# Row chunks of the adaLN product in pairs, with five places, and shift columns loaded two tiles ahead

## The chip, the cores and the metric

The kernel runs on one core of a Trainium2 chip. The metric is the time of one execution on the device in microseconds (us); the lower the better. TensorE (PE) multiplies matrices, VectorE (DVE), ScalarE (ACT) and GpSimd (POOL) work on vectors, SyncE (SP) issues transfers; DMA engines move the data.

## What is computed

Two decoder layers on 256 positions of width 2048, in float32. Layer 0 has a causal conformer convolution as token mixer, layer 1 a stick-breaking attention; both are followed by a gated MLP. Each part is normed, shifted, scaled and gated by numbers that a conditioning vector c gives through its own product (adaLN). What matters here is the middle of layer 0:

```python
def ada_ln(c, w, b):
    mod = jax.nn.silu(c) @ w + b
    shift, scale, gate = jnp.split(mod, 3, axis=-1)

def conformer_conv_module(h, ...):
    u = h @ pw1_w + pw1_b
    ...
    u = causal_depthwise_conv(u, dw_w, dw_b)
    u = jax.nn.silu(layer_norm(u, ln_g, ln_b))
    return u @ pw2_w + pw2_b
...
    x = x + gate * y
    shift, scale, gate = ada_ln(c, ffn_mod_w[i], ffn_mod_b[i])
    h = rms_norm(x, ffn_norm_g[i]) * (1.0 + scale) + shift
    x = x + gate * conv_ffn(h, ffn_up_w[i], ffn_dw_w[i], ffn_dw_b[i], ffn_down_w[i])
```

## The kernel before, in words

A large product is made of blocks of 128 x 128 weights. The weights are split in two parts, wh and wl, and so is the input (zh, zl in this stage), and each block takes three matmuls (L297 to L299) on 256 columns. Weights come in pieces of eight blocks (0.5 MB), loaded by SP (L225), split by ACT (L243) and DVE (L247). The stage of this study is pw2, the second product of the conv module, with 32 pieces, 768 matmuls. Its inputs are the 16 results of the conv (ys, tiles of 128 x 256): DVE subtracts the mean (L922), multiplies by the deviation (L923), ACT and DVE make zh and zl. The first eight output tiles run interleaved over the first twelve input tiles and are then finished one by one; the last eight run one by one. Finished output tiles are evicted by ACT (L941), added to x by DVE (L942), and squared and summed for the next norm by ACT (L392) and POOL (L396).

Beside it runs a filler, a generator that the loop over pieces advances by a step after each piece. It computes adaLN numbers that later stages need, in two ways. Row chunks, 128 x 2048 numbers (1 MB): a chunk is multiplied on PE by four matmuls of 32 columns by 512, on four column groups at once (L576; the trace shows two records for each), and its rows are turned and biased later (L592, L598). Forty chunks make the gate of layer 0's mixer (0 to 15), the scale of its MLP (16 to 31) and half its shift (32 to 39). Chunks 20 to 39 are loaded in the pw2 stage by POOL (L556), each when PE has read what was in its place. The places are tiles of 1 MB: three named mraw and one zrow, given out by number and capped. The other half of the shift is made from columns tiles (mraw, 1 MB, loaded by `mod_load`, L318), each multiplied with silu(c) and summed by DVE in one instruction (L330, 2.3 us).

A scheduler of the framework fixes one order of instructions per engine from the program's text; up to the end of the conv the order is written out by hand, and in pw2 it is the scheduler's. Each engine works through its list in order, so that a load on POOL's list waits for what stands ahead of it. A place is used again when the reading of it is over, by a semaphore.

Of the kernel before, what the change touches and what calls it, by code (L numbers as in the profile page):

```python
# [10 lines left out]
F32 = mybir.dt.float32  # L11
# [5 lines left out]
P = 128  # L17
# [14 lines left out]
MORE_ROWS = 4  # L32
SPLIT_ROWS = 3
ROWS = 2

ROWS_AT = {**{c: (11,) for c in (2, 4, 6, 8, 10, 12)}, 13: (16, 17), 14: (8, 12, 16), 15: (2, 13, 15, 17)}
ROWS_TAIL = 5

RATES = {"pw2": (1.0, 0.0), "up": (0.44, 0.25), "down": (0.5, 0.0), "qk": (0.3, 0.0), "v": (0.3, 0.0),
         "o": (0.45, -3.0), "up00a": (0.0, 0.0), "qk0a": (0.0, 0.0),  # L40
# [76 lines left out]
def hybrid_trunk(ctx: ExitStack, tc: tile.TileContext, cfg: Cfg, io: dict):  # L117
    nc = tc.nc
    D, T, H = cfg.D, cfg.T, cfg.H
# [198 lines left out]
    def mod_load(m, nb, own=False):  # L318

        v = mpool.tile([P, D], F32, name="mraw")  # L320
        src = io["mt_" + m][mt_at[m].index(nb) if m in mt_at else nb]
        if own:
            nc.gpsimd.dma_start(v, src)  # L323
        else:
            load(src, v)
        return v

    def mod_reduce(m, nb, v):

        nc.vector.tensor_tensor_reduce(out=v, in0=v, in1=csr, scale=1.0, scalar=0.0, op0=ALU.mult, op1=ALU.add,  # L330
                                       accum_out=macc[:, nb:nb + 1])
# [11 lines left out]
    def mod_part(m, part, first):  # L343
        ahead = []
        for nb in range(part * KD + first, (part + 1) * KD):
            ahead.append((nb, mod_load(m, nb)))
            if len(ahead) > 1:
                mod_reduce(m, *ahead.pop(0))
            yield
        mod_reduce(m, *ahead.pop(0))  # L350
        mod_sum(m, part * KD + first, KD - first)
        yield

    later = []

# [139 lines left out]
    with ExitStack() as cv:  # L495
# [39 lines left out]
        def load_rows(most=1):  # L535

            while row_chunks and most:
                n = nrow["n"]
                near = n < nrow["near"]
                home = row_homes[n] if near else ("zmm"[n % 3] if n < 8 * KD // 4 else "zm"[n % 2]) if "z" in cpar else "m"  # L540
                cap = {"m": 3 if near else 1 + (n < 8 * KD // 4), "r": MORE_ROWS, "w": SPLIT_ROWS, "z": 1}[home]
                if sum(t[1] == home for t in row_tiles) >= cap:
                    break
                m, c, k0 = row_chunks.pop(0)
                src = io["mr_" + m][mr_at[m].index(c), :, k0 * 512:(k0 + 4) * 512]
                if home == "w":
                    v = [w_pool.tile([P, PW], F32R, name=x).bitcast(F32) for x in ("wh", "wl")]
                    for i in range(2):
                        load(src[:, i * PW:(i + 1) * PW], v[i])
                    v = [v[g // 2][:, g % 2 * 512:(g % 2 + 1) * 512] for g in range(4)]  # L550
                else:
                    v = (cpool2.tile([P, 4 * 512], F32, name="mrow", bufs=MORE_ROWS) if home == "r" else
                         cpar["z"].tile([P, 4 * 512], F32, name="zrow") if home == "z" else
                         mpool.tile([P, 4 * 512], F32, name="mraw"))
                    if "z" in cpar:
                        nc.gpsimd.dma_start(v, src)  # L556
                    else:
                        load(src, v)
                    v = [v[:, g * 512:(g + 1) * 512] for g in range(4)]
                row_tiles.append((v, home))  # L560
                nrow["n"] += 1
                most -= 1

        def mod_rows():
# [4 lines left out]
            for m, c0, n, done in rows_of:  # L569
                ps = (psum_acc if m == "ffn0" and c0 else psum_a)() if n else None  # L570
                for i in range(n):
                    for k0 in range(0, KD, 4):
                        v = row_tiles.pop(0)[0]
                        first, last = i == 0 and k0 == 0, i == n - 1 and k0 + 4 >= KD
                        for g in range(4):
                            nc.tensor.matmul(ps[32 * g:32 * g + 32, :], hot[:, k0 + g, 31 - i:63 - i],  # L576
                                             v[g], start=first, stop=last,
                                             tile_position=(0, 32 * g))
                        load_rows()
                        if later and nrow["bias"]:  # L580
                            later.pop(0)()
                        if last:
                            rows = cpool.tile([P, 512], F32, name="rows")
                            nc.scalar.copy(rows, ps)
                        else:
                            yield
# [18 lines left out]
                yield  # L605

        def mods0():
            part = mod_part("ffn0", 0, 4 * cfg.rows0) if cfg.rows0 * 4 < KD else iter(())
            for _ in mod_rows():
                yield  # L610
                if ("ffn0", 1) in have and next(part, "end") != "end":
                    yield
            yield from part
            have.add(("ffn0", 0))

        gb = cpool.tile([P, KD], F32, name="gb")
        ready = {"k": 0}
        ys = [cpool.tile([P, T], F32, name=f"y{j}") for j in range(KD)]
        for kt in range(KD):
            nc.gpsimd.tensor_tensor(ys[kt], xs[kt], rs, op=ALU.mult)  # L620
        htiles = [h_tiles(kt) for kt in range(KD)]
# [678 lines left out]
```

## Time and profile before

| | us |
|---|---|
| median of three runs | 2310.33 (2307.93 to 2311.91) |
| the profiled execution | 2314.76 |
| its span, first to last instruction | 2313.1 |
| stage pw2 in it, first to last matmul | 286.5 to 408.9 |

The profile shows one execution. Its own time lies above the span by what is outside the first and last instruction. The rows below come from the page and from questions to its trace: timelines (one engine's instructions, with start, duration and in brackets the idle time ahead of it and what ended it), groups by line, waits, windows, and how long transfers took from issue to landing.

### The profile page before, as it was taken

What the parts mean: (1) busy time and instruction counts of PE and PEld (TensorE: products, weight loads), DVE (VectorE), ACT (ScalarE), POOL (GpSimd) and SP (SyncE); (2) the same over time, 40 slices, a digit from 0 to 9 for tenths busy, and PEclk for the clock granted to TensorE, in tenths of its full rate; (3) what the DMA queues carried; (4) which work ended last, traced back from release to release, by engine and by line L of the source; (5) the groups of instructions that cost most, each with busy time, mean ns of one, the idle gap of its engine ahead of it and who ended that gap; (6) DMA issues with size and microseconds to landing.
All of it is one profiled execution on the core that took longest, in us unless ns stands there. A gap on an engine that the chain in (4) does not pass through costs nothing.

```text
span 2313.1 us, 44241 instructions
## 1 busy us (share of the span) xinstructions
PE 2273.3 (98%) x17834; PEld 2170.2 (94%) x17834; DVE 1737.9 (75%) x2386; ACT 1163.5 (50%) x1776; POOL 334.4 (14%) x478
## 2 busy tenths in 40 slices
PE   7999999999999999999999999999999999999997
PEld 5888678999999999999999999999999999999997
DVE  7689968899998899998875555668666545666554
ACT  2056655755543355554465555647555434555543
POOL 4058713200001000001211000121000000000010
PEclk9999999999999999999999999999999999999999
DMA  9988798689999999998854555555555555555553
GB/s 394 417 323 308 272 370 350 236 319 362 344 362 386 361 343 358 348 357 329 330 182 164 165 172 174 164 191 177 189 191 186 189 187 187 190 186 190 188 186 110
DMA packets 139167, 603.56 MB, mean 261 GB/s; under 512 B 15441, under 2 KB 15569, under 8 KB 115153
## 3 DMA queue, kind: packets, MB, share of 16 engines
q1 hardware_dynamic: 120242, 464.42, 56.0%
q0 software_dynamic: 18720, 136.32, 15.8%
q8 instruction: 139, 2.28, 0.4%
q14 instruction: 66, 0.54, 0.1%
HBM read 598.58 MB, written 2.10 MB: 260 GB/s over the span
## 4 chain that ended last, share of the span: by engine, by line
PE 62%; issue 23%; DVE 5%; DMA 5%; POOL 2%; ACT 1%; POOLq 0%; SPq 0%; DVEq 0%; ACTq 0%
PE ps L297 17%; PE ps L298 17%; PE ps L299 16%; PE ps L663 5%; DMA mraw<-in_mt_mix 3%; POOL mraw L323 2%; DVE mraw L330 2%; DMA mraw<-in_mt_ffn 2%; DVE wl L247 1%; PE ps L1125 1%; PE ps L1127 1%; PE ps L1126 1%; PE ps L576 1%; PE auxa L576 1%; ACT hl L712 0%
## 5 line engine op out<-in xcount | busy, mean ns | idle before, releaser
L247 DVE TENSOR_TENSOR wl<-raw,wh 128x1024 fp32r<-128x1024 f32 x688 | 844.4, 1231 | 414.7 <-ACT wh L243 409.1
L243 ACT CAST wh<-raw 128x1024 fp32r<-128x1024 f32 x688 | 719.3, 1048 | 822.9 <-PE ps L298 645.9
L297 PE MATMUL ps<-hh,wh 128*128 128x256 f32 (+1 forms) x3264 | 915.8, 281 | 0.0
L298 PE MATMUL ps<-hl,wh 128*128 128x256 f32 (+1 forms) x3264 | 912.1, 279 | 0.0
L299 PE MATMUL ps<-hh,wl 128*128 128x256 f32 (+1 forms) x3264 | 908.3, 278 | 0.1
L298 PEld LDWEIGHTS ps<-hl,wh 128*128 128x128 f32 x3264 | 617.7, 189 | 0.3
L299 PEld LDWEIGHTS ps<-hh,wl 128*128 128x128 f32 x3264 | 612.8, 188 | 0.7 <-DVE wl L247 0.7
L297 PEld LDWEIGHTS ps<-hh,wh 128*128 128x128 f32 x3264 | 612.7, 188 | 0.3
L299 PE MATMUL ps<-gh,wl 128*128 128x256 f32 x1408 | 394.6, 280 | 7.1 <-DVE wl L247 7.1
L298 PE MATMUL ps<-gl,wh 128*128 128x256 f32 x1408 | 396.4, 282 | 0.0
L297 PE MATMUL ps<-gh,wh 128*128 128x256 f32 x1408 | 395.4, 281 | 0.0
L330 DVE CUSTOM_DVE_ANT_0 mraw<-mraw,csr 128x2048 f32<-128x2048 f32 x152 | 348.5, 2294 | 52.6 <-DMA mraw<-in_mt_mix 30.9
L299 PEld LDWEIGHTS ps<-gh,wl 128*128 128x128 f32 x1408 | 266.0, 189 | 8.1 <-DVE wl L247 8.1
L298 PEld LDWEIGHTS ps<-gl,wh 128*128 128x128 f32 x1408 | 266.9, 190 | 0.0
L297 PEld LDWEIGHTS ps<-gh,wh 128*128 128x128 f32 x1408 | 266.2, 189 | 0.0
L396 POOL TENSOR_TENSOR sumsq<-sumsq,t 128x256 f32<-128x256 f32 x56 | 65.0, 1162 | 885.8 <-ACT t L392 885.6
L663 PE MATMUL ps<-hh,raw 128*128 128x256 f32 x832 | 188.8, 382 | 0.0
L663 PEld LDWEIGHTS ps<-hh,raw 128*128 128x128 f32 x832 | 157.8, 191 | 28.3 <-issue 6.7
L964 DVE SCALAR_TENSOR_TENSOR t<-ps,par,t 128x254 f32<-128x254 f32 x328 | 157.1, 479 | 3.9
L703 DVE SCALAR_TENSOR_TENSOR auxb<-u,cpar,auxb 128x256 f32<-128x256 f32 x297 | 121.6, 483 | 4.5 <-ACT auxb L687 3.7
L838 POOL TENSOR_TENSOR y<-y,hl 128x256 f32<-128x256 f32 x143 | 104.4, 730 | 13.4 <-ACT hl L712 3.3
L961 ACT ACTIVATE t<-ps,par 128x256 f32<-128x256 f32 x164 | 91.8, 560 | 0.0
(247 smaller groups left out, 2271.3 us busy)
## 6 DMA issues: line engine op xcount, KB each, us to landing
raw<-in_w_down SPq DMA_DIRECT2D x176, 512.0 KB, 3.8
mraw<-in_mt_ffn POOLq DMA_DIRECT2D x64, 1024.0 KB, 8.3
raw<-in_w_pw SPq DMA_DIRECT2D x96, 512.0 KB, 7.9
mraw<-in_mt_mix POOLq DMA_DIRECT2D x48, 1024.0 KB, 8.1
raw<-in_w_up01b SPq DMA_DIRECT2D x84, 512.0 KB, 6.8
raw<-in_w_up11b SPq DMA_DIRECT2D x84, 512.0 KB, 3.5
raw<-in_w_up00b SPq DMA_DIRECT2D x80, 512.0 KB, 6.5
raw<-in_w_up10b SPq DMA_DIRECT2D x80, 512.0 KB, 3.5
```

What stands on the lines that cost most here:

```text
L243: nc.scalar.copy(wh[:, :n], v[:, :n])
L247: nc.vector.tensor_tensor(wl[:, :n], v[:, :n], wh[:, :n].bitcast(F32), op=ALU.subtract)
L297: nc.tensor.matmul(o, wh[:, c], xh[kt], start=first, stop=False, skip_group_check=halves > 0)
L298: nc.tensor.matmul(o, wh[:, c], xl[kt], start=False, stop=False, skip_group_check=halves > 0)
L299: nc.tensor.matmul(o, wl[:, c], xh[kt], start=False, stop=left[nb] == 0, skip_group_check=halves > 0)
L330: nc.vector.tensor_tensor_reduce(out=v, in0=v, in1=csr, scale=1.0, scalar=0.0, op0=ALU.mult, op1=ALU.add, accum_out=macc[:, nb:nb + 1])
L396: engine.tensor_tensor(self.sum, self.sum, sq, op=ALU.add)
L663: nc.tensor.matmul(banks[j][:, nb // KD * T:(nb // KD + 1) * T], w[:, b * P:(b + 1) * P], hf[kt], start=first, stop=left[j] == 0, skip_gro ...
L703: nc.vector.scalar_tensor_tensor(conv_ps[j], us[j % UBUFS][:, k:k + T], tap(j, k), conv_ps[j], op0=ALU.mult, op1=ALU.add)
L838: nc.gpsimd.tensor_tensor(ys[c], ys[c], pr, op=ALU.add)
L961: nc.scalar.activation(y, ps[:, :T], AF.Identity, bias=pc(f"fdb{i}", nb, 1), scale=w(FW - 1))
L964: nc.vector.scalar_tensor_tensor(y[:, s:], ps[:, :T - s], w(k), y[:, s:], op0=ALU.mult, op1=ALU.add)
```

## The change

The places of chunks 20 to 39 come from a string, `LATE_HOMES`, with one letter for each chunk: m (two tiles mraw), z (zrow), y (two halves of what held the conv's results). The results ys are now cut from two tiles of eight results, named yhalf, and a chunk with home y takes a half when its results have been read. In the pw2 stage the filler takes two row chunks at a step, and two loads are issued at a chunk in place of one; two columns tiles stand behind each pair once the scale is done. Columns tiles of the shift are loaded by POOL (`own=True`) in place of SP, and two tiles are in flight ahead of the one that is reduced, in place of one.

```diff
@@ -35,6 +35,8 @@
 
 ROWS_AT = {**{c: (11,) for c in (2, 4, 6, 8, 10, 12)}, 13: (16, 17), 14: (8, 12, 16), 15: (2, 13, 15, 17)}
 ROWS_TAIL = 5
+
+LATE_HOMES = "mmzyymmzyymzyyzyyzyy"
 
 RATES = {"pw2": (1.0, 0.0), "up": (0.44, 0.25), "down": (0.5, 0.0), "qk": (0.3, 0.0), "v": (0.3, 0.0),
          "o": (0.45, -3.0), "up00a": (0.0, 0.0), "qk0a": (0.0, 0.0),
@@ -343,13 +345,14 @@
     def mod_part(m, part, first):
         ahead = []
         for nb in range(part * KD + first, (part + 1) * KD):
-            ahead.append((nb, mod_load(m, nb)))
-            if len(ahead) > 1:
+            ahead.append((nb, mod_load(m, nb, own=True)))
+            if len(ahead) > 2:
                 mod_reduce(m, *ahead.pop(0))
+                yield
+        while ahead:
+            mod_reduce(m, *ahead.pop(0))
             yield
-        mod_reduce(m, *ahead.pop(0))
         mod_sum(m, part * KD + first, KD - first)
-        yield
 
     later = []
 
@@ -537,8 +540,8 @@
             while row_chunks and most:
                 n = nrow["n"]
                 near = n < nrow["near"]
-                home = row_homes[n] if near else ("zmm"[n % 3] if n < 8 * KD // 4 else "zm"[n % 2]) if "z" in cpar else "m"
-                cap = {"m": 3 if near else 1 + (n < 8 * KD // 4), "r": MORE_ROWS, "w": SPLIT_ROWS, "z": 1}[home]
+                home = row_homes[n] if near else LATE_HOMES[n - nrow["near"]] if "z" in cpar else "m"
+                cap = {"m": 3 if near else 2, "r": MORE_ROWS, "w": SPLIT_ROWS, "z": 1, "y": 2}[home]
                 if sum(t[1] == home for t in row_tiles) >= cap:
                     break
                 m, c, k0 = row_chunks.pop(0)
@@ -551,6 +554,7 @@
                 else:
                     v = (cpool2.tile([P, 4 * 512], F32, name="mrow", bufs=MORE_ROWS) if home == "r" else
                          cpar["z"].tile([P, 4 * 512], F32, name="zrow") if home == "z" else
+                         cpool.tile([P, 4 * 512], F32, name="yhalf", bufs=2) if home == "y" else
                          mpool.tile([P, 4 * 512], F32, name="mraw"))
                     if "z" in cpar:
                         nc.gpsimd.dma_start(v, src)
@@ -576,7 +580,7 @@
                             nc.tensor.matmul(ps[32 * g:32 * g + 32, :], hot[:, k0 + g, 31 - i:63 - i],
                                              v[g], start=first, stop=last,
                                              tile_position=(0, 32 * g))
-                        load_rows()
+                        load_rows(2 if nrow["bias"] else 1)
                         if later and nrow["bias"]:
                             later.pop(0)()
                         if last:
@@ -605,17 +609,26 @@
                 yield
 
         def mods0():
+
             part = mod_part("ffn0", 0, 4 * cfg.rows0) if cfg.rows0 * 4 < KD else iter(())
-            for _ in mod_rows():
+            rows = mod_rows()
+            while next(rows, "end") != "end":
+                if nrow["bias"]:
+                    next(rows, "end")
+                    yield
+                    for _ in range(2 if ("ffn0", 1) in have else 0):
+                        next(part, "end")
+                        yield
                 yield
-                if ("ffn0", 1) in have and next(part, "end") != "end":
-                    yield
-            yield from part
+            for _ in part:
+                yield
+                yield
             have.add(("ffn0", 0))
 
         gb = cpool.tile([P, KD], F32, name="gb")
         ready = {"k": 0}
-        ys = [cpool.tile([P, T], F32, name=f"y{j}") for j in range(KD)]
+        yhalf = [cpool.tile([P, KD // 2 * T], F32, name="yhalf", bufs=2) for _ in range(2)]
+        ys = [yhalf[j * 2 // KD][:, j % (KD // 2) * T:(j % (KD // 2) + 1) * T] for j in range(KD)]
         for kt in range(KD):
             nc.gpsimd.tensor_tensor(ys[kt], xs[kt], rs, op=ALU.mult)
         htiles = [h_tiles(kt) for kt in range(KD)]
```

In the changed kernel L297 to L299 become L299 to L301, L576 is L580, L556 is L560, L396 is L399, L922 is L935, L941 is L954 and L942 is L955.

**Row chunks on PE.** In the first quarter of the stage, PE's list before has a chunk (L576) alone between groups of 24 matmuls:

```order
443 L297 MATMUL ps<-zh_2271,wh 128x256
444 L298 MATMUL ps<-zl_2272,wh 128x256
445 L299 MATMUL ps<-zh_2271,wl 128x256
446 L576 MATMUL ps<-mraw,hot 32x512 x4
447 L297 MATMUL ps<-zh_2283,wh 128x256
448 L298 MATMUL ps<-zl_2284,wh 128x256
449 L299 MATMUL ps<-zh_2283,wl 128x256
```

The list after has a run of four chunks (24, 25, 26, 27) after a longer stretch of matmuls; yhalf, mraw and zrow are places:

```order
598 L300 MATMUL ps<-zl_2322,wh 128x256
599 L301 MATMUL ps<-zh_2321,wl 128x256
600 L299 MATMUL ps<-zh_2329,wh 128x256
601 L580 MATMUL ps<-yhalf,hot 32x512 x4
602 L580 MATMUL ps<-mraw,hot 32x512 x8
603 L580 MATMUL ps<-zrow,hot 32x512 x4
604 L300 MATMUL ps<-zl_2330,wh 128x256
605 L301 MATMUL ps<-zh_2329,wl 128x256
606 L299 MATMUL ps<-zh_2329,wh 128x256
```

Over the stage 13 runs of chunks stand where there were 22. In matmuls of pw2 between the runs: chunk 20 in two parts with 21 behind it, 24, part of 22, 24, rest of 22, 101, chunk 23, 44, chunks 24 to 27, 20, chunk 28, 46, chunks 29 to 31, then 32 and 33 in two runs within 29 matmuls, 84, chunks 34 and 35, 108, chunks 36 and 37, 96, chunks 38 and 39. From chunk 39 on 168 matmuls follow.

**Loads on POOL.** POOL's list before, from the end of the conv (chunks 20 and on):

```order
201 L556 DMA mraw<-in_mr_ffn 128x2048
202 L556 DMA zrow<-in_mr_ffn 128x2048
203 L556 DMA mraw<-in_mr_ffn 128x2048 x4
204 L556 DMA zrow<-in_mr_ffn 128x2048
205 L556 DMA mraw<-in_mr_ffn 128x2048 x2
206 L556 DMA zrow<-in_mr_ffn 128x2048
207 L556 DMA mraw<-in_mr_ffn 128x2048
208 L556 DMA zrow<-in_mr_ffn 128x2048
209 L556 DMA mraw<-in_mr_ffn 128x2048
210 L556 DMA zrow<-in_mr_ffn 128x2048
```

The list after at the same place, with what each waits for (a tile's number says which allocation it is; DVE or PE is the engine that must have read the place, DMASW a transfer into it, or into its queue):

```order
193 L560 DMA mraw_2427<-in_mr_ffn0 128x2048 [waits DMAHW4_49,DMAHW0_49,PE_49]
194 L560 DMA zrow_2413<-in_mr_ffn0 128x2048 [waits DMAHW3_49,DMAHW5_49,DMAHW2_49,DMAHW6_49,DMAHW0_49,DMAHW7_49,DVE_49,PE_49]
195 L560 DMA mraw_2495<-in_mr_ffn0 128x2048 [waits DMAHW7_49,PE_49]
196 L560 DMA mraw_2575<-in_mr_ffn0 128x2048 [waits DMAHW4_49,DMAHW0_49,PE_49]
197 L560 DMA zrow_2497<-in_mr_ffn0 128x2048 [waits DMASW1_49,PE_49]
198 L560 DMA yhalf_2415<-in_mr_ffn0 128x2048 [waits DVE_49]
199 L560 DMA yhalf_2425<-in_mr_ffn0 128x2048 [waits DMASW5_49,PE_49]
200 L560 DMA yhalf_2503<-in_mr_ffn0 128x2048 [waits DMASW6_49,PE_49]
201 L560 DMA zrow_2645<-in_mr_ffn0 128x2048 [waits DMASW4_49,DMASW0_49,PE_49]
202 L560 DMA yhalf_2569<-in_mr_ffn0 128x2048 [waits DMASW7_49,PE_49]
203 L560 DMA yhalf_2711<-in_mr_ffn0 128x2048 [waits DMASW2_49,DVE_49]
204 L560 DMA yhalf_2717<-in_mr_ffn0 128x2048 [waits DMASW3_49,DMASW1_49,PE_49]
```

Loads of chunks 23, 24, 28, 29 are the first four of yhalf. The first waits for DVE, each following one for PE's reading, and for the transfer of the one before; the fifth, chunk 32, waits for DVE again, which means the other half.

**The shift's columns.** Later in POOL's list before, sums of squares (L396) and row loads alternate:

```order
211 L396 TENSOR_TENSOR sumsq<-sumsq,t 128x256 x4
212 L556 DMA mraw<-in_mr_ffn 128x2048
213 L396 TENSOR_TENSOR sumsq<-sumsq,t 128x256 x2
214 L556 DMA zrow<-in_mr_ffn 128x2048
215 L396 TENSOR_TENSOR sumsq<-sumsq,t 128x256 x3
216 L556 DMA mraw<-in_mr_ffn 128x2048
217 L556 DMA zrow<-in_mr_ffn 128x2048
```

After, loads of columns tiles (L325, from in_mt_ffn) stand between the sums, and chunk 39's load (yhalf) is behind the tenth sum, counted from the stage's start:

```order
207 L399 TENSOR_TENSOR sumsq<-sumsq,t 128x256
208 L560 DMA yhalf<-in_mr_ffn 128x2048
209 L399 TENSOR_TENSOR sumsq<-sumsq,t 128x256
210 L325 DMA mraw<-in_mt_ffn 128x2048
211 L399 TENSOR_TENSOR sumsq<-sumsq,t 128x256
212 L325 DMA mraw<-in_mt_ffn 128x2048
213 L399 TENSOR_TENSOR sumsq<-sumsq,t 128x256
214 L560 DMA yhalf<-in_mr_ffn 128x2048
```

In the list of DVE before, the second reduction (L330) stands behind the second add to x (L942), the first one ahead of all adds:

```order
522 L942 TENSOR_TENSOR x<-x,t 128x256
523 L449 SCALAR_TENSOR_TENSOR hl_2864<-x,a_ffn_2860,hh_2863 128x256
524 L247 TENSOR_TENSOR wl<-raw,wh 128x1024
525 L942 TENSOR_TENSOR x<-x,t 128x256
526 L330 ISA mraw,macc<-mraw,csr 128x2048
527 L330 ISA macc 128x1
528 L449 SCALAR_TENSOR_TENSOR hl_2886<-x,a_ffn_2860,hh_2885 128x256
529 L942 TENSOR_TENSOR x<-x,t 128x256
```

After, the first two stand behind the sixth and seventh adds (L955):

```order
532 L955 TENSOR_TENSOR x<-x,t 128x256
533 L332 ISA mraw,macc<-mraw,csr 128x2048
534 L332 ISA macc 128x1
535 L452 SCALAR_TENSOR_TENSOR hl_2994<-x,a_ffn_2848,hh_2993 128x256
536 L955 TENSOR_TENSOR x<-x,t 128x256
537 L332 ISA mraw,macc<-mraw,csr 128x2048
538 L332 ISA macc 128x1
539 L452 SCALAR_TENSOR_TENSOR hl_3025<-x,a_ffn_2848,hh_3024 128x256
```

The loads of these columns moved from SP (L225) to POOL (L325); the conv stage's list and those of later stages keep their order.

## Rows read from the trace of the kernel before

**Rows 1.** Page, part 1: busy us (share of the span) and instructions of each engine.

```profile
PE 2273.3 (98%) x17834; PEld 2170.2 (94%) x17834; DVE 1737.9 (75%) x2386; ACT 1163.5 (50%) x1776; POOL 334.4 (14%) x478
```

**Rows 2.** Windows of the pw2 stage: us, busy times, granted clock, DMA share, GB/s.

```profile
286.50:408.90 122.40, 120.25 (x952) 98.52 (x951) 92.40 (x146) 68.94 (x127) 26.76 (x30) 1.00 0.92 356
...
286.00:300.00 14.00, 14.00 (x101) 10.31 (x102) 8.76 (x18) 7.63 (x13) 1.05 (x2) 1.00 0.79 282
300.00:345.00 45.00, 45.00 (x358) 34.48 (x353) 30.85 (x53) 24.95 (x42) 5.29 (x10) 1.00 1.00 398
...
365.00:395.00 30.00, 30.00 (x248) 26.12 (x248) 25.18 (x29) 15.67 (x26) 8.70 (x8) 1.00 1.00 401
```

**Rows 3.** Groups by line in 286.5 to 408.9 on PE: busy, mean ns, idle before.

```profile
L297 PE MATMUL ps<-zh,wh 128*128 128x256 f32 x256 | 74.2, 291 | 2.1 <-ACT t L941 2.1
```

**Rows 4.** PE's waits, 286 to 409: total, times, longest.

```profile
PE ps L297 <- ACT t L941: 2.1, 2, 1.6
```

**Rows 5.** PE's timeline: start, us, operation; a chunk alone among pw2 matmuls.

```profile
292.55 0.39 PE L297 MATMUL ps<-zh,wh 128*128 128x256 f32 x1
...
295.37 0.28 PE L299 MATMUL ps<-zh,wl 128*128 128x256 f32 x1
295.58 1.07 PE L576 MATMUL ps<-mraw,hot 128*32 128x512 f32 x8
296.57 0.39 PE L297 MATMUL ps<-zh,wh 128*128 128x256 f32 x1
296.80 0.28 PE L298 MATMUL ps<-zl,wh 128*128 128x256 f32 x1
```

**Rows 6.** PE's timeline: where pw2 waited for an eviction.

```profile
353.62 0.39 PE L297 MATMUL ps<-zh,wh 128*128 128x256 f32 x1 [1.60 <-ACT t L941]
...
359.73 0.38 PE L297 MATMUL ps<-zh,wh 128*128 128x256 f32 x1 [0.55 <-ACT t L941]
```

**Rows 7.** PE's timeline: chunks one behind another, ahead of the stage.

```profile
281.26 1.07 PE L576 MATMUL auxa<-mrow,hot 128*32 128x512 f32 x8
282.15 1.04 PE L576 MATMUL ps<-mrow,hot 128*32 128x512 f32 x8
283.00 0.60 PE L576 MATMUL ps<-wh,hot 128*32 128x512 f32 x2
```

**Rows 8.** POOL's timeline: a row load's issue and two sums of squares.

```profile
296.95 0.53 POOL L556 DMA_DIRECT2D mraw<-in_mr_ffn  x1 [5.45 <-PE ps L576]
...
352.86 0.72 POOL L396 TENSOR_TENSOR sumsq<-sumsq,t 128x256 f32<-128x256 f32 x1 [1.21 <-ACT t L392]
...
378.66 2.13 POOL L396 TENSOR_TENSOR sumsq<-sumsq,t 128x256 f32<-128x256 f32 x1 [1.57 <-ACT t L392]
```

**Rows 9.** DVE's timeline: reading of result 7; reduction of a shift tile.

```profile
306.75 0.43 DVE L923 TENSOR_TENSOR t<-y,rstd 128x256 f32<-128x256 f32 x1
...
346.87 2.29 DVE L330 CUSTOM_DVE_ANT_0 mraw<-mraw,csr 128x2048 f32<-128x2048 f32 x1 [2.38 <-DMA mraw<-in_mt_ffn]
```

**Rows 10.** Chunk loads (L556) issued in 275:400, 283:298, 300:327, 355:366, 374:378.

```profile
DMA to landing us min/median/max: 5.2/8.2/10.3
...
DMA to landing us min/median/max: 5.7/6.0/8.0
...
DMA to landing us min/median/max: 8.2/8.6/9.4
...
DMA to landing us min/median/max: 5.2/5.9/6.7
...
DMA to landing us min/median/max: 8.6/9.5/10.3
```

**Rows 11.** DVE's waits, 286 to 409, on shift tiles: total, times, longest.

```profile
DVE mraw L330 <- DMA mraw<-in_mt_ffn: 9.7, 4, 4.0
```

**Rows 12.** ACT's timeline: the eviction of output tile 10.

```profile
376.04 0.55 ACT L941 ACTIVATE t<-ps,gb,v_mix 128x256 f32<-128x256 f32 x1
```


## The prediction

> **What bounds the kernel now.** I first read the page's busy shares: TensorE (PE) is busy 98% of the span [rows 1], so time is won or lost only where it waits or switches between kinds of work. The change touches the stage of the conv's second product (pw2), which runs from 286.5 to 408.9 us. The windows come next: in this stage PE is busy 120.25 of 122.40 us, at a granted clock of 1.00, and the DMA engines stand at a share of 1.00 in two long stretches, with 398 and 401 GB/s [rows 2]. The groups by line give the 768 matmuls of pw2 (256 for each of three lines) [rows 3], and the list of waits gives the only thing PE waits for there: 2.1 us in two places, on ACT's eviction of a finished output tile [rows 4, 6]. PE waits for no weights and for no row chunk. The bound is PE's own instruction stream, and the cover for the loads is thin where DMA is full.
>
> **What joining chunks removes.** In PE's order before, row chunks (four column groups of L576) stand singly between 24 or more pw2 matmuls. The timeline shows such a place: last matmul at 295.37, chunk at 295.58, next matmuls at 296.57 and 296.80 [rows 5]. From 295.37 to 296.80 are 1.43 us; the pitch of plain matmuls is 0.118 (23 steps from 292.55 to 295.37, less 0.11 for the longer first one), so two pitches (0.24) would have passed anyway, and a lone chunk costs 1.19 us. A chunk that follows a chunk costs less: 281.26, 282.15, 283.00 are two steps in 1.74 us, 0.87 each [rows 7]. Each join so saves 0.32 us. By the order after, the stage's chunks stand in 13 runs where there were 22, which is nine joins, **-2.9 us**. The two waits on the eviction go back to DVE: the reduction of a shift tile at 346.87 waits 2.38 us for its load and then takes 2.29 [rows 9], with DVE's add of the output tile behind it, ACT's square of that sum behind the add, and the next eviction behind the square. The order after puts the first two reductions behind the adds of tiles 5 and 6 (before: ahead of the first, and behind the second), so the evictions that PE waited for come earlier, and I count the waits as gone: **-2.1 us** (0 if they return later). The floor is -5.0 us.
>
> **What the new places add.** The order after says that the five places are four at first. Chunks 23, 24, 28 and 29 each wait for PE's reading of the one before among them: they share one half of the conv's results, and the other half is first used by chunk 32. So a chain begins that the kernel before did not have: PE reads a chunk, POOL issues the next load, the load lands, PE may read again. PE does other pw2 matmuls meanwhile, and stalls for what is left. Call the time from issue to landing L. POOL issued 0.31 us after the end of the reading in the trace (reading ends at 295.58 + 1.07 = 296.65, issue at 296.95) [rows 5, 8], so the landing is 1.06 + 0.31 + L = L + 1.37 after the previous chunk's first matmul.
> Chunk 23: its half is free when DVE has read result 7, at 306.75 + 0.43 [rows 9], so it is issued near 307.5. PE comes to it after 24, 24 and 101 matmuls and one chunk counted from 292.55 [rows 5]: 292.55 + 149 x 0.118 + 1.7 (the chunk, in two runs) + 0.2 = 312.0. The stall is L - 4.5.
> Chunk 24: 44 matmuls further, 0.99 + 5.2 + 0.2 = 6.4 after the first matmul of 23; stall L + 1.37 - 6.4 = L - 5.0.
> Chunk 28: a run of four chunks (0.99 + 3 x 0.87), 20 matmuls (2.4) and 0.2 make 6.2; stall L - 4.8.
> Chunk 29: 0.99 + 46 x 0.118 + 0.2 = 6.6; stall L - 5.25.
> Together 4L - 19.6 us, wherever L is above 5.25. PE waits with everything behind it: the pw2 matmuls in its queue can't pass the chunk.
> L has no single value: 5.2 to 10.3 us over all chunks, with a median of 8.2 [rows 10]. At 300 to 327, the stretch of the chain, the median was 8.6, but there before issued a 1 MB chunk for every 24 matmuls into a full DMA [rows 2, 10]. Pieces of weights alone (0.52 MB in each of 32 pieces, 122.4 us) are 137 GB/s of the 398. With the chain, one chunk goes out in 6 or 7 us in place of 4, so its load meets less traffic. The rows of light traffic (283 to 298 with a mean of 282 GB/s, and 355 to 366) have medians of 6.0 and 5.9 [rows 2, 10]. I take L = 6.0, since that condition is nearer to the chain's: **+4.4 us**, with +1.3 at 5.2 (three of the four links then still stall) and +13.2 at 8.2 as the ends.
> The Trainium skill, page "DMA: Bandwidth & Descriptors", section "Anatomy of one DMA — SWDGE (gpsimd) path", gives for a load issued by GpSimd a fit of 2.0 us and its bytes over 436 KB per us; as an estimate that is 4.4 us for a chunk of 1 MiB. By that no link of the chain would stall, and the sum would end at the floor. The lowest of the trace here is 5.2, so the measurement decides here.
>
> **What moving the shift's columns adds.** Before, the eight tiles of shift columns (1 MB each) were loaded by SP between weights; now POOL issues them, two ahead, and POOL works in order. Queued among them are the sums of squares (L396) and the row loads 36 to 39. On the gain side DVE waited 9.7 us for these tiles [rows 11], which PE never felt [rows 4], so two ahead wins nothing on the path. On the cost side stands chunk 39: its load is behind the tenth sum of squares, which in the trace ran from 378.66 for 2.13 us, to 380.8, 4.8 us after the eviction of output tile 10 began at 376.04 [rows 8, 12]. PE needs chunk 39 after 72 matmuls and chunk 38, 8.5 + 0.2 + 1.0 = 9.7 us after that tile's end. The stall is L - 4.9. Here the traffic is the heavy kind (401 GB/s) [rows 2], and the loads issued at 374 to 378 took 8.6 to 10.3 [rows 10]; I take the lower, 8.6: **+3.7 us**, between +0.3 (5.2) and +5.4 (10.3).
> The reductions of tiles 8 and 9 now precede the low part of weight piece 19 in DVE's order, and their loads stand behind sums of squares, for the second one that ran at 352.86 for 0.7 us [rows 8]. With L of 5.9 it lands near 359.5 and is reduced (2.3) by 362, which the matmuls of the piece (three pieces after 353.62, near 364) [rows 6] cover; at 8.2 it is some 1.5 late. I take 0, range to +1.5. The conv stage and all later stages have the same order as before, and their term is 0. Bytes moved are the same.
>
> **The sum.** -2.9 - 2.1 + 4.4 + 3.7 = **+3.1 us** against the profiled execution (span 2313.1, whole 2314.76). That execution lies 4.4 above the median of 2310.33, within a spread of runs that is no property of the stage, so I put the difference on the median: 2313.4, given as 2313. A measurement of this kernel can tell 0.2% (4.6 us) from no change.
>
> **The rivals.**
> *The chain decides (slower).* One half serves four chunks, and the price is 4L - 19.6 - 5.0 with chunk 39's term on top. With that at 3.7, the total passes +4.6 from L = 6.4 in the chain. At L = 8.2, near what 300 to 327 shows, it is +13.2 + 3.7 - 5.0 = +11.9: 2322. For it: the stretch was full before. Against it: the chain itself thins the traffic.
> *Loads land in time (faster).* If landings in the chain and at chunk 39 take under 4.5 us, only the floor is left, -5.0: 2305. This is also where the skill's fit leads. For it: fewer loads in flight than ever in the trace. Against it: no chunk of this stage landed under 5.2, and at 5.2 everywhere the sum is -5.0 + 1.3 + 0.3 = -3.4, 2307, which counts as no change.
> *Joining saves nothing.* If a run of several chunks costs 1.19 for each, as lone ones do, the -2.9 is missing and the forecast becomes +6.0: 2316. Rows 7 speak against it, though on chunks of other places.
>
> **How the numbers follow.** Forecast (L between 5.2 and 6.4 in the chain; -3.4 to +4.6) 0.50; chain decides 0.28; joins save nothing 0.06; loads in time 0.16. So faster 0.16, same 0.50, slower 0.34. The range reaches from just above the floor, 2306, to near the slower rival, 2321.
>
> **What would show it.** In the profile after: PE's waits in pw2 list the row chunks' DMA at L580, some four short ones between 312 and 345 and one near 385, of 1 us each in the first and 4 in the last; the waits on the eviction are gone; chunk loads into the halves show 5 to 7 us. The windows of the stage would sum to about 125.5 us. I'd be wrong if these waits were absent (landings faster than any seen), if they were 3 us or more each, if PE's waits named the low part of weights (DVE late), or if time moved in a stage outside pw2.

## The result, and the profile after

The changed kernel takes 2321.98 us (median, 2317.95 to 2323.51), the kernel before in the same comparison 2310.55: a ratio of 1.0049, 95% interval 1.0039 to 1.0059. It is slower by 11.4 us. The forecast was 2313 in a range of 2306 to 2321; the time lies just above the range, and at what the first rival gave, 2322.

The profiled execution took 2323.51 us, with a span of 2321.8. The page's first part answers [rows 1]; PE has the same work:

```profile
PE 2274.0 (98%) x17834; PEld 2171.0 (94%) x17834; DVE 1737.6 (75%) x2386; ACT 1164.6 (50%) x1776; POOL 335.0 (14%) x486
```

The windows answer [rows 2]: us, then busy time of PE, PEld, DVE, ACT, POOL, the granted clock, the DMA share and GB/s. The first line is the pw2 stage, the others are stretches of 4 us in it:

```profile
285.80:420.90 135.10, 122.59 (x951) 100.68 (x951) 92.71 (x146) 69.25 (x127) 27.72 (x38) 0.96 0.86 323
...
316.00:320.00 4.00, 3.93 (x19) 2.29 (x20) 0.95 (x3) 0.00 (x0) 0.53 (x1) 0.57 0.53 169
340.00:344.00 4.00, 4.00 (x24) 0.88 (x16) 0.00 (x0) 0.00 (x0) 0.53 (x1) 0.57 0.85 287
398.00:402.00 4.00, 4.00 (x23) 2.84 (x16) 1.46 (x2) 0.58 (x1) 0.00 (x0) 0.57 1.02 418
```

The stage now takes 135.1 us in place of 122.4, 12.7 more; it starts 0.8 earlier. In the stretches behind 316, 340 and 398 the granted clock is 0.57 in the mean: for more than three quarters of each, PE ran at the lower of its two levels, 1.2 GHz. Before it was 1.00 in the whole stage [rows 2]. The two spans differ by 8.7 us only: from the stage's end to the last instruction, the profiled execution of the kernel before took 1904.2 us and that of the changed kernel 1900.9. Of these 3.3 us, 1.7 are clock, near 1140, where both ran for a while at the lower level.

PE's waits in the stage (total, times, longest) answer [rows 4]; ps and auxa are buffers that PE writes to:

```profile
PE ps L580 <- DMA yhalf<-in_mr_ffn: 6.8, 3, 4.0
PE auxa L580 <- DMA yhalf<-in_mr_ffn: 3.7, 1, 3.7
PE ps L301 <- DVE wl L249: 1.9, 2, 1.5
```

The 2.1 us on the eviction are gone. In their place stand 10.5 us on chunks in the conv's halves, and 1.9 on the low part of weights (wl). The timeline of PE (start, us, operation, idle ahead of it) shows the first of these waits, chunk 23:

```profile
316.07 1.87 PE L580 MATMUL ps<-yhalf,hot 128*32 128x512 f32 x8 [4.03 <-DMA yhalf<-in_mr_ffn]
317.87 0.58 PE L301 MATMUL ps<-zh,wl 128*128 128x256 f32 x1
...
318.46 0.42 PE L300 MATMUL ps<-zl,wh 128*128 128x256 f32 x1
318.68 0.42 PE L301 MATMUL ps<-zh,wl 128*128 128x256 f32 x1
...
319.81 0.28 PE L301 MATMUL ps<-zh,wl 128*128 128x256 f32 x1
319.93 0.28 PE L299 MATMUL ps<-zh,wh 128*128 128x256 f32 x1
```

PE idles for 4.03 us. Then the chunk takes from 316.07 to 317.87, 1.80 us where a lone chunk took 0.99 [rows 5], and the pitch of the pw2 matmuls behind it is 0.21 us; at 319.81 it is back at 0.12. The low clock costs 1.6 us here (3.6 for what takes 2.05 at the full one).

Chunks 24 to 27 show what joining does; the first and the last of the run:

```profile
324.04 1.07 PE L580 MATMUL ps<-yhalf,hot 128*32 128x512 f32 x8
...
326.64 1.04 PE L580 MATMUL ps<-zrow,hot 128*32 128x512 f32 x8
```

Three steps in 2.60 us are 0.87 each, as in [rows 7].

The same view of POOL shows the issues of chunk 23 and of chunk 39; then, for chunks 23, 24, 29 and 39 in this order, the time from issue to landing (answers to [rows 8, 10]); chunk 28 took 5.1 like chunk 24:

```profile
306.65 0.53 POOL L560 DMA_DIRECT2D yhalf<-in_mr_ffn  x1 [5.92 <-DVE t L936]
...
388.73 0.57 POOL L560 DMA_DIRECT2D yhalf<-in_mr_ffn  x1
```

```profile
DMA to landing us min/median/max: 9.4/9.4/9.4
...
DMA to landing us min/median/max: 5.1/5.1/5.1
...
DMA to landing us min/median/max: 7.4/7.4/7.4
...
DMA to landing us min/median/max: 8.9/8.9/8.9
```

### The profile page after: what moved, and what is told of

It is laid out like the page before. It is cut to its first block, busy times and chain, and to the rows that moved or that the text cites. A ratio compares the mean times of both kernels' runs of the same rounds, so it can differ in the third digit from the quotient of the medians.

```text
span 2321.8 us, 44236 instructions
## 1 busy us (share of the span) xinstructions
PE 2274.0 (98%) x17834; PEld 2171.0 (94%) x17834; DVE 1737.6 (75%) x2386; ACT 1164.6 (50%) x1776; POOL 335.0 (14%) x486
## 3 DMA queue, kind: packets, MB, share of 16 engines
q8 instruction: 139, 2.28, 0.4%
## 4 chain that ended last, share of the span: by engine, by line
PE 84%; DMA 6%; DVE 6%; issue 2%; ACT 1%; POOL 0%; DVEq 0%; SPq 0%; POOLq 0%; ACTq 0%
PE ps L299 24%; PE ps L300 24%; PE ps L301 24%; PE ps L676 5%; DMA mraw<-in_mt_mix 3%; DVE mraw L332 2%; DMA mraw<-in_mt_ffn 2%; DMA yhalf<-in_mr_ffn 2%; DVE wl L249 1%; PE ps L1138 1%; PE ps L1140 1%; PE ps L1139 1%; PE ps L580 1%; PE auxa L580 0%; DVE hl L384 0%
## 5 line engine op out<-in xcount | busy, mean ns | idle before, releaser
L299 PE MATMUL ps<-hh,wh 128*128 128x256 f32 (+1 forms) x3264 | 917.3, 281 | 0.0
L301 PE MATMUL ps<-hh,wl 128*128 128x256 f32 (+1 forms) x3264 | 909.4, 279 | 0.1
L301 PEld LDWEIGHTS ps<-hh,wl 128*128 128x128 f32 x3264 | 613.7, 188 | 0.7 <-DVE wl L249 0.7
L299 PEld LDWEIGHTS ps<-hh,wh 128*128 128x128 f32 x3264 | 613.3, 188 | 0.3
L301 PE MATMUL ps<-gh,wl 128*128 128x256 f32 x1408 | 394.6, 280 | 5.0 <-DVE wl L249 5.0
L299 PE MATMUL ps<-gh,wh 128*128 128x256 f32 x1408 | 395.4, 281 | 0.0
L332 DVE CUSTOM_DVE_ANT_0 mraw<-mraw,csr 128x2048 f32<-128x2048 f32 x152 | 348.5, 2294 | 44.6 <-DMA mraw<-in_mt_mix 31.0
L301 PEld LDWEIGHTS ps<-gh,wl 128*128 128x128 f32 x1408 | 265.9, 189 | 5.8 <-DVE wl L249 5.8
L299 PEld LDWEIGHTS ps<-gh,wh 128*128 128x128 f32 x1408 | 266.0, 189 | 0.0
L399 POOL TENSOR_TENSOR sumsq<-sumsq,t 128x256 f32<-128x256 f32 x56 | 61.8, 1104 | 885.5 <-ACT t L395 885.3
L716 DVE SCALAR_TENSOR_TENSOR auxb<-u,cpar,auxb 128x256 f32<-128x256 f32 x297 | 121.6, 482 | 4.5 <-ACT auxb L700 3.7
L851 POOL TENSOR_TENSOR yhalf<-yhalf,hl 128x256 f32<-128x256 f32 x143 | 104.4, 730 | 13.4 <-ACT hl L725 3.3
```

The source lines that it names most:

```text
L299: nc.tensor.matmul(o, wh[:, c], xh[kt], start=first, stop=False, skip_group_check=halves > 0)
L301: nc.tensor.matmul(o, wl[:, c], xh[kt], start=False, stop=left[nb] == 0, skip_group_check=halves > 0)
L399: engine.tensor_tensor(self.sum, self.sum, sq, op=ALU.add)
L716: nc.vector.scalar_tensor_tensor(conv_ps[j], us[j % UBUFS][:, k:k + T], tap(j, k), conv_ps[j], op0=ALU.mult, op1=ALU.add)
L851: nc.gpsimd.tensor_tensor(ys[c], ys[c], pr, op=ALU.add)
```

## The experiments

The prediction's first rival became the theory, with one addition that the trace had brought: PE waits for chunks whose place is the one half of the conv's results, and behind long waits it runs at the lower clock. The rivals: the columns on POOL cost it, or the runs of chunks do.

**The places as before.**

```diff
-home = ... LATE_HOMES[n - nrow["near"]] if "z" in cpar else "m"
+home = ... ("zmm"[n % 3] if n < 8 * KD // 4 else "zm"[n % 2]) if "z" in cpar else "m"
-cap = {"m": 3 if near else 2, ...
+cap = {"m": 3 if near else 1 + (n < 8 * KD // 4), ...
```

> Pairs and the columns on POOL as in the change; chunks 20 to 39 take their places as before (three places, each conv result its own tile's use only). Theory (waits for chunks whose place is one half of the conv's results, and PE's lower clock behind long waits): the waits on yhalf's transfers, 10.5 us in the trace after, and the stretches at a clock under 1.00 go, the joins and the eviction's end stay: 2304 to 2309, under the kernel before. Rival (the columns behind POOL's sums, or long runs of chunks, cost it): stays at 2315 to 2322.

Measured: 2314.01 us, ratio 1.0019 (1.0010 to 1.0028), between theory and rival and 1 us under the rival's 2315. The waits on the halves are gone and with them 8 us; the rest of the theory's number was too good. PE's three longest waits (the list has 1.0 more) and the stage's window:

```profile
PE auxa L580 <- DMA zrow<-in_mr_ffn: 3.0, 1, 3.0
PE ps L580 <- DMA zrow<-in_mr_ffn: 2.0, 1, 2.0
PE ps L299 <- ACT t L954: 1.1, 1, 1.1
```

```profile
285.70:415.40 129.70, 122.67 (x951) 101.28 (x951) 91.21 (x144) 66.97 (x124) 27.07 (x37) 0.96 0.85 330
```

Pairs in the old three places wait too, for zrow, and the clock mean of 0.96 says that this costs its part again. The trace is of the longest of eleven executions, 5.0 us above their median.

**The columns as before.**

```diff
-ahead.append((nb, mod_load(m, nb, own=True)))
-if len(ahead) > 2:
+ahead.append((nb, mod_load(m, nb)))
+if len(ahead) > 1:
```

> Pairs and the five places as in the change; the shift's columns loaded by SP, one ahead, as before. Theory: the three waits of the chain (6.8 us) and the lower clock behind two of them (some 3.5) stay, the wait for chunk 39 and the 1.9 us on the low weights shrink or go: 2312 to 2318. Rival (the columns on POOL are the cause): 2304 to 2309.

Measured: 2323.59 us, ratio 1.0061 (1.0048 to 1.0075). Against the rival: putting the columns back gains nothing. It lies above the theory's range too. PE's waits and the stage's window:

```profile
PE ps L579 <- DMA yhalf<-in_mr_ffn: 9.3, 3, 4.5
PE ps L299 <- ACT t L953: 4.0, 1, 4.0
```

```profile
285.70:422.10 136.40, 123.10 (x951) 100.90 (x951) 92.31 (x146) 69.14 (x127) 22.22 (x30) 0.95 0.85 320
```

The waits of the chain stay (9.3), the one for chunk 39 is gone as expected, where the load has one sum of squares fewer ahead of it. The eviction takes its place with 4.0 us: DVE waits for tiles of the shift, ahead of the adds that ACT needs:

```profile
DVE mraw L332 <- DMA mraw<-in_mt_ffn: 14.8, 4, 5.6
```

**The pairs alone.** The two edits above together.

> Only the pairs: two chunks at a step, two loads at a chunk; places and columns as before. Theory: joins save about 3 us and nothing waits: 2305 to 2310. Rival (a run of chunks costs as much as lone ones, or pairs wait for their loads in three places): 2310 to 2316.

Measured: 2311.55 us, ratio 1.0009 (1.0000 to 1.0018): about level, in the rival's range, and by the rival's second form: pairs wait for their loads in three places. The trace is of the shortest of eleven executions, 2.3 us under their median. PE's waits, the stage's window, and in the timeline the longest of the waits:

```profile
PE ps L579 <- DMA zrow<-in_mr_ffn: 2.3, 1, 2.3
PE auxa L579 <- DMA zrow<-in_mr_ffn: 1.5, 2, 1.0
```

```profile
285.80:407.40 121.60, 117.86 (x951) 98.46 (x951) 90.24 (x145) 67.97 (x127) 23.34 (x30) 1.00 0.91 354
```

```profile
317.67 1.07 PE L579 MATMUL ps<-zrow,hot 128*32 128x512 f32 x8 [2.27 <-DMA zrow<-in_mr_ffn]
318.67 0.39 PE L299 MATMUL ps<-zh,wh 128*128 128x256 f32 x1
```

The stage takes 121.6. Waits for zrow of 3.8 us eat most of what the joins and the vanished eviction (2.1) give. There are eight joins here, as one chunk comes in two parts: 8 x 0.32 = 2.6, and 122.4 - 2.6 - 2.1 + 3.8 = 121.5. The wait of 2.27 us left no slow stretch (the chunk behind it takes 1.00).

These kernels separate the causes. With the pairs made, the new places cost 12.0 us on columns as before (2311.55 to 2323.59) and 8.0 on moved ones (2314.01 to 2321.98); moving the columns shows nothing clear of the intervals (+2.5 on the old places, -1.6 on the new ones).

**The columns alone**, on the kernel before (the `mod_part` of the change, nothing else).

> The kernel before with one part: the shift's columns loaded by POOL, two ahead. Theory: within 2 us of the kernel before, with PE's 2.1 us on the eviction gone or less: 2307 to 2312. Rival (loads behind POOL's sums come late and hold DVE, so PE waits for low weights): 2313 to 2317.

Measured: 2313.16 us, ratio 1.0014 (1.0005 to 1.0023), a little above the theory's range and at the low end of the rival's, but not by the rival's mechanism: PE doesn't wait for the low part of weights. It waits longer for the eviction (and the mean clock in the stage is 0.99):

```profile
PE ps L297 <- ACT t L942: 3.3, 2, 2.3
```

**Half the bytes.** In the changed kernel, chunks in the halves were loaded with half of their columns.

```diff
+if home == "y":
+    nc.gpsimd.dma_start(v[:, :2 * 512], src[:, :2 * 512])
...
+v = [... for g in ((0, 1, 0, 1) if home == "y" else range(4))]
```

> The changed kernel, but a chunk in one of the conv's halves is loaded with only the first 1024 of its 2048 columns, and its four matmuls read those twice (the adaLN numbers are not those of the reference). Everything else of the change stays. Theory: landings in the chain fall from 5.1-9.4 us to 3-6, the waits on yhalf (10.5 us) fall under 3, the granted clock stays at 1.00 behind them, and the time comes to 2305 to 2312. Rival (pairs, places and the columns cost PE something that is not this wait): 2316 or more.

Measured: 2313.44 us, ratio 1.0014 (1.0005 to 1.0022), 8.5 us under the changed kernel, though above the theory's range. The waits on the halves fall from 10.5 to 4.7, not under 3, 3.1 on the eviction come in, and the clock still falls (0.97 in the mean). The waits of PE, and the landings of chunks 23 and 24:

```profile
PE ps L582 <- DMA yhalf<-in_mr_ffn: 4.7, 2, 3.5
PE ps L299 <- ACT t L956: 3.1, 2, 2.5
```

```profile
DMA to landing us min/median/max: 7.3/7.3/7.3
...
DMA to landing us min/median/max: 3.9/3.9/3.9
```

Chunk 24 takes 3.9 us in place of 5.1. Chunk 23, at half its bytes, still takes 7.3 in place of 9.4, so most of its time is not that of its own bytes. PE's wait for it falls by 0.5 only (4.0 to 3.5), since the scheduler has moved it, too: it stands behind 88 matmuls, not 101, and PE comes to it earlier.

**Work in the wait.** Is it PE's idleness that brings the low clock? Chunk 23 was held back in the program, without and with 34 further matmuls ahead of it.

```diff
+if nrow["used"] == 23:
+    for _ in range(HELD):
+        yield
+    d = psum_b() if FILL else None
+    for f in range(FILL):
+        nc.tensor.matmul(d[:, :T], zs[0][0][:, :P], zs[0][0], ...)
```

> The changed kernel with chunk 23 held back by four steps of the filler, so that it is written behind the pw2 matmuls that run ahead of it anyway. The control for the next one: PE comes to chunk 23 near 312 and waits some 4 us for it, as in the changed kernel, and the clock falls to 1.2 GHz behind the wait (both theories).

> The same with 34 further matmuls of 128 x 256 (zh by zh, into a spare bank, 4.0 us at a pitch of 0.118, their result not used) ahead of chunk 23: work added where PE would wait. Theory (the idle of PE lowers its clock): the load lands at the same time near 316, PE idles under 1 us, the granted clock stays at 1.00 there, and chunk 23 and the matmuls behind it take some 1.8 us less, counted from the chunk's first matmul to the 24th pw2 matmul behind it, 3.9 against 5.5 us; the kernel with more work is no slower, or faster by up to 2 us. Rival (matmuls behind a landing are slow for another reason, like the transfers in flight): the slow stretch stays as long as in the control, and the added work shows nothing or costs time.

Measured: 2322.09 without, 2320.07 with the added matmuls, ratios 1.0052 (1.0037 to 1.0067) and 1.0041 (1.0027 to 1.0055); the intervals overlap. Chunk 23 in the timeline of the control, then of the kernel with added work:

```profile
315.60 1.06 PE L588 MATMUL ps<-yhalf,hot 128*32 128x512 f32 x8 [3.48 <-DMA yhalf<-in_mr_ffn]
316.59 0.39 PE L302 MATMUL ps<-zh,wl 128*128 128x256 f32 x1
```

```profile
315.47 1.07 PE L588 MATMUL ps<-yhalf,hot 128*32 128x512 f32 x8
316.46 0.39 PE L300 MATMUL ps<-zh,wh 128*128 128x256 f32 x1
```

The control failed: behind an idle time of 3.48 us the clock did not fall (the chunk takes 0.99 us). So the pair says nothing on the clock at this place. It does show that the wait has room for some 4 us of further work: chunk 23 starts at 315.47 in place of 315.60. Elsewhere in the control, behind a wait of 2.67 us that ends at 338.34, the clock did fall.

The other kernels' traces settle a part. In the fourteen traces PE has 24 waits of 1.99 us or more in the stage. At 20 of them the granted clock fell to the lower level, during the wait or within 1.6 us behind it; at four it did not (2.06, 2.07, 2.27 and 3.48 us). No slow stretch came without such a wait. And a landing isn't needed: it fell as well behind waits on ACT's eviction, like one of 3.42 us ahead of 350.49 in `late_halves_yy` (the next kernel below):

```profile
350.00:354.00 4.00, 3.51 (x18) 3.51 (x19) 1.72 (x3) 2.01 (x4) 1.63 (x3) 0.57 0.93 367
```

So the rival, that matmuls are slow behind a landing, falls, and PE's idleness stands as the cause, by where the stretches lie and not by an experiment. Which of the waits bring the clock down stays open.

**Better places.** From here on the question was whether pairs can beat the kernel before. First, the halves only from chunk 32 on, with three tiles mraw before that and the columns on SP:

```diff
-LATE_HOMES = "mmzyymmzyymzyyzyyzyy"
+LATE_HOMES = "mmzmmmzmmmzmyyzyyzyy"
-cap = {"m": 3 if near else 2, ...
+cap = {"m": 3 if n < 32 else 1, ...
```

> Pairs; the columns on SP, one ahead, as before; the halves of the conv's results take chunks only from 32 on, and three tiles mraw serve up to chunk 31 (in place of two). Theory: no place is read and loaded again within the stretch that PE needs for less than 48 matmuls and a run, so PE waits under 2 us in the stage and the clock stays at 1.00: 122.3 less 2.9 (joins) less up to 2.1 in the stage, 2305 to 2308, faster than the kernel before. Rival (pairs gain nothing): 2310 to 2313.

> As the kernel with the halves from chunk 32 on, but these chunks go over both halves, zrow and one mraw in turn (four places), so that a load has a whole pair more time. Theory: the same 2305 to 2308, with no wait for chunk 39; a load in mraw waits for DVE's reduction of a shift tile and holds the two behind it on POOL, which may cost up to 2 us. Rival: 2310 to 2313.

The second has "mmzmmmzmmmzmyyzmyyzm" and its cap changes at 31. Measured: 2313.27 us, ratio 1.0015 (1.0006 to 1.0024), and 2319.39, ratio 1.0034 (1.0021 to 1.0046). Both miss. PE's waits in the first and in the second (which has 1.3 more on the low part of weights):

```profile
PE ps L299 <- ACT t L953: 3.9, 2, 3.4
PE ps L579 <- DMA mraw<-in_mr_ffn: 1.8, 2, 1.2
```

```profile
PE ps L299 <- ACT t L953: 8.6, 2, 5.1
PE ps L579 <- DMA mraw<-in_mr_ffn: 2.3, 2, 1.6
```

No chunk waits for long any more, but the eviction does. DVE's timeline of the second shows why:

```profile
343.89 2.29 DVE L332 CUSTOM_DVE_ANT_0 mraw<-mraw,csr 128x2048 f32<-128x2048 f32 x1 [13.09 <-DMA mraw<-in_mt_ffn]
...
348.55 0.42 DVE L954 TENSOR_TENSOR x<-x,t 128x256 f32<-128x256 f32 x1
```

The reduction of a shift tile (L332) waited 13.09 us for its load with the adds (L954) behind it in DVE's list, and the next reduction (2.28 us) follows the first add.

**The columns later.** In the next two the columns begin two pairs later, once on the pairs alone, once on the late halves; in the last one they begin at the filler's seventeenth step in the kernel before.

```diff
-for _ in range(2 if ("ffn0", 1) in have else 0):
+for _ in range(2 if ("ffn0", 1) in have and nrow["pair"] >= 9 else 0):
```

> As pairs_alone (places as before, columns on SP, one ahead), but the shift's columns begin two pairs later, behind chunks 36 and 37. Theory: DVE's reductions then stand behind the adds of output tiles 5 and 7, so no eviction comes late: PE waits only for zrow (2 to 4 us), the clock stays at 1.00, 2306 to 2311. Rival (columns begun late end late, and the next stage waits for the shift): 2312 or more.

> As late_halves_yy (halves from chunk 32 on, three tiles mraw up to 31), with the columns two pairs later. Theory: the 3.9 us on the eviction and the lower clock behind them (1.5) go, 1.8 us of waits for mraw stay: 2306 to 2309, at or under the kernel before. Rival (columns late, or chunk 39 late behind POOL's sums): 2312 or more.

> The kernel before with one part changed that the study points to: the shift's columns begin later, from the seventeenth step of the filler in the stage, so that DVE's first reduction stands behind the fourth add of an output tile in place of ahead of all. Single chunks, places and queues as before. Theory: the 2.1 us on the eviction go, nothing else waits, the clock stays at 1.00: 2306 to 2310, 1 to 3 us under the kernel before. Rival (PE waits for chunks or low weights in their place): 2311 or more.

Measured: 2312.93 (ratio 1.0017, 1.0008 to 1.0026), 2313.15 (1.0011, 1.0002 to 1.0020) and 2313.53 (1.0012, 1.0003 to 1.0021). All miss. PE's waits in the three, in this order (the second has 2.6 more on two late chunks, the third 0.4 more on an eviction):

```profile
PE auxa L579 <- DMA zrow<-in_mr_ffn: 4.5, 3, 2.1
PE ps L579 <- DMA zrow<-in_mr_ffn: 2.1, 1, 2.1
```

```profile
PE ps L299 <- ACT t L954: 2.5, 1, 2.5
PE ps L579 <- DMA mraw<-in_mr_ffn: 1.4, 2, 1.1
```

```profile
PE auxa L577 <- DMA zrow<-in_mr_ffn: 4.2, 2, 3.0
```

In the first, the eviction no longer waits, as the theory says of DVE's order, but zrow is waited for 6.6 us; in the last, 4.2 us on zrow take the place of 2.1 on the eviction. The scheduler shifts runs and loads with each edit, and in each of these kernels something new comes late. No version beat the kernel before.

**All of them in one sum.** Stage and clock are the window's (low clock: 1 less the mean granted clock, times the stage; its two digits leave 0.6 us open), waits are PE's listed waits in the stage:

| kernel | chunks | stage | waits | low clock | rest |
|---|---|---|---|---|---|
| before | single | 122.4 | 2.1 | 0 | 120.3 |
| cols_alone | single | 125.1 | 3.3 | 1.3 | 120.5 |
| singles_cols_later | single | 126.8 | 4.6 | 3.8 | 118.4 |
| after | pairs | 135.1 | 12.4 | 5.4 | 117.3 |
| places_undone | pairs | 129.7 | 7.1 | 5.2 | 117.4 |
| cols_undone | pairs | 136.4 | 13.3 | 6.8 | 116.3 |
| pairs_alone | pairs | 121.6 | 3.8 | 0 | 117.8 |
| half_rows | pairs | 128.0 | 7.8 | 3.8 | 116.4 |
| late_halves_yy | pairs | 124.5 | 5.7 | 1.2 | 117.6 |
| late_halves | pairs | 132.8 | 12.2 | 5.3 | 115.3 |
| pairs_cols_later | pairs | 123.3 | 6.6 | 0 | 116.7 |
| halves_cols_later | pairs | 126.1 | 6.5 | 3.8 | 115.8 |
| held | pairs | 130.7 | 11.5 | 3.9 | 115.3 |
| held_filled | pairs | 133.9 | 9.4 | 4.0 | 120.5 |

Of the last row's rest, 4.0 are the added matmuls; in both held kernels eight small matmuls (1 us) lie outside the stage. Without these two rows the rest is 119.7 in the mean with single chunks and 116.7 with pairs: 3.0 us, what eight or nine joins should save. But it runs from 118.4 to 120.5 in the one group and from 115.3 to 117.8 in the other, so the table bears out the size of the joins only roughly; the step of 0.87 us within a run says it more directly. The differences of 8 us and more between stages are waits and the clock behind them. These are single profiled executions; the medians above are the measure of the kernels.

## Why the prediction was wrong

**Right, with its size.** The joins (-2.9; a step of 0.87 within a run, the table's rest some 3 lower), the end of the eviction's waits (-2.1; none in the list after), and the chain itself: chunks 23, 24, 28 and 29 wait for one place, by the formulas of the prediction. With the measured landings they give 9.4 - 4.5 = 4.9, 5.1 - 5.0 = 0.1, 5.1 - 4.8 = 0.3 and 7.4 - 5.25 = 2.2, in sum 7.5; PE's waits were 4.0, none, some 0.5 and 2.3, in sum 6.8. The first is lower since chunk 23 was issued at 306.65, not 307.5. Chunk 39 was given 8.6 - 4.9 = 3.7 and waited 3.7; that it fits to the tenth is luck, as the landing took 8.9 and PE came 5.2 us after the issue.

**The first failed step: L = 6.0 for all four links.** For chunks 24 and 28 it was, if anything, too high (5.1 each). It failed for chunk 23, which landed in 9.4 us and made PE wait 4.0 where the prediction had 1.5, and for chunk 29 (7.4; 2.3 where it had 0.75). The argument was that fewer chunk loads leave DMA less full. SP's queue (q1, which carries the weights) shows what happened: its packets, MB and share of the DMA engines, before while a chunk issued at 305.10 was under way (8.6 us), then after, during chunk 23 (9.4 us) and chunk 24 (5.1 us):

```profile
q1 hardware_dynamic: 381, 1.41, 40.7%
```

```profile
q1 hardware_dynamic: 709, 2.58, 68.7%
...
q1 hardware_dynamic: 10, 0.03, 1.6%
```

Before, the weights moved at 163 GB/s there, not far from the 137 that I had reckoned from the mean of the stage. During chunk 23 they moved at 275, and the total was the same 411 GB/s in both stretches: pieces of weights, already issued, took the share that the chunks gave up (their time from issue to landing fell from 14.7 us to 7.2). With half the bytes in chunk 23 they moved 2.24 MB in 7.3 us, 307 GB/s, and the total was 403. Chunk 24 then met a queue that was almost empty, for SP issued no piece between 313.70 and 323.42. Chunk 29's load had chunk 32's beside it, which POOL issued 0.6 us later, since the change issues two at a time. The row that was nearest in time, [rows 10] for 300 to 327 with 8.2 to 9.4, was the right one for chunk 23, and I had set it aside for all four by an argument on traffic.

**The second failed step: no term for the clock.** The sum took PE's pace as given, since the granted clock was 1.00 [rows 2]. In the profile after it falls behind the waits of 4.0, 2.3 and 3.7 us, and three stretches at 1.2 GHz cost 4.8 us by the timelines (1.6 behind chunk 23), 5.4 by the mean clock. That is the largest single piece of the miss; the chain's waits are 2.4 of it (6.8 for 4.4). The Trainium skill, page "TensorE: Matmul & The Clock Gate", section "HAM oscillation — how this bites in real kernels", describes this: waits on DMA between products let the clock fall, and the next work starts at the lower level. At these three waits the trace agrees; at the wait of 3.48 us in the control, and that of 2.27 with the pairs alone, it did not fall.

**A third, small one.** The waits for the low part of weights: +1.9 where I had 0 up to +1.5.

The sum by what was measured: -2.9 - 2.1 + 6.8 + 3.7 + 1.9 + 5.4 = +12.8 (12.2 with the clock's 4.8), against 12.7 in the stage. The fit of the Trainium skill, page "DMA: Bandwidth & Descriptors", section "Anatomy of one DMA — SWDGE (gpsimd) path", weighed in the prediction for a load by GpSimd, gave an estimate of 4.4 us for such a chunk, and with it no wait at all; the lowest landing after was 5.1, so the measurement decided rightly there.

**The rivals.** The one that came about was priced at 2322 by a landing of 8.2 in all links. Its time was right by luck, by errors that cancel: the chain's waits came to 6.8, not 13.2, while the clock (some 5) and the low part of weights (1.9) were missing. "Joining saves nothing" fell by the steps of 0.87 us within a run. "Loads land in time" fell by the landings. The columns, which I had held for harmless but for chunk 39, cost 1.4 thousandths when made alone.

## What to carry to other kernels

When a buffer is used again, ask which use frees it and write down the chain: end of reading, issue, landing, next reading; two places that come free at different times act as one until the later one is free. Take the landing time from the rows at that place and time, and ask what else the queues carry there, before an argument on thinner traffic may lower it: another queue with work in hand can take what the first one gives up. And where a busy TensorE gets waits of some microseconds, add a term for the slower pace behind them: here it came to some 5 us beside 12.4 us of waits.

## What the runs showed of the hardware

A chunk of 1 MB took 5.1 us from issue to landing where SP's queue moved 0.03 MB beside it, and 9.4 where it moved 2.58 MB; halving its bytes took 1.2 us off the first kind (5.1 to 3.9) and 2.1 off the second (9.4 to 7.3). With fewer chunk loads under way the total stayed at 411 GB/s, and the weights' part rose from 163 to 275. Behind waits of 2.3, 3.7 and 4.0 us TensorE ran at the lower level for about 3.4 us each (a granted clock of 0.57 over 4 us), with a pitch of 0.21 in place of 0.12, which cost 1.6 to 1.7 us; behind one of 3.48 us in another kernel it stayed up. The length of the wait alone doesn't decide, and what does was not settled.
